# One maximum per head in the global attention branch, copies and sums moved between engines, and an output product that begins with the first tokens

## The chip, the cores and the metric

The kernel runs on one core of a Trainium2 chip. The metric is the device time of one execution in microseconds. The kernel before took 1566.17 us (median of three runs, 1564.94 to 1567.08). The engines are named as the profile names them: PE (TensorE), PEld (its weight loads), DVE (VectorE), ACT (ScalarE), POOL (GpSimd) and SP (SyncE, which here only starts DMAs).

## What is computed

One layer of a diffusion transformer over 1024 latent tokens of width 1024 with 256 context tokens. Two attention branches read the same modulated input: A, windowed over 128 neighbours with a sink logit, and B, global, with a normalisation of q and k. Each has 8 query heads in two groups of four (one key/value head per group), head size 64. A SwiGLU convolution network follows. What the change touches is branch B and the merge:

```python
def _global_attention(q, k_all, v_all):          # keys: 1024 latent + 256 context
    def one_block(i):
        q_blk = lax.dynamic_slice_in_dim(q, i * BLOCK, BLOCK, axis=1)
        p = jax.nn.softmax(_gqa_scores(q_blk, k_all), axis=-1)
        return _gqa_values(p, v_all)
...
def _merge_branches(o_a, o_b, gate_logits, w_branch_a, w_branch_b, w_out):
    g_a, g_b = jnp.split(jax.nn.sigmoid(gate_logits), 2, axis=-1)
    return (g_a * (o_a @ w_branch_a) + g_b * (o_b @ w_branch_b)) @ w_out
```

## The kernel before

All is float32. Every product of a weight with an activation is made of three matmuls on rounded halves (high and low part of each operand, `mm3`, lines 92 to 95; `split`, lines 83 to 90, makes the halves: a rounding copy and a subtraction).

The kernel is a sequence of stages: the projections and gates (to about 336 us of the profile), the attention (to about 764 us), the output product of branch B and the merge (to about 812 us), the output projection with its layer norm, and the convolution network (to the end). The attention goes over 32 units. A unit is one branch, one block of 128 query tokens and one group of four heads; units 0 to 15 are branch A, units 16 to 31 branch B (in the names of tiles, `p_6_1_3` is block 6, group 1, head 3).

A unit of branch B has two parts. The score part: `context` (lines 550 to 553) makes the scores against the 256 context keys for four heads in one PSUM tile `s_x` (`cxp`, lines 501 to 514), DVE takes their maximum (L508, L509), and ACT makes the four exponentials from PSUM (L463 with tile `p_x`). Then `lat` (lines 465 to 499) makes for each head the scores against the 1024 latent keys in another PSUM tile, DVE copies them out scaled and keeps their extreme with the context maximum as the start value (L496), and ACT makes the exponential in place. So the context part has one maximum, and the latent part another that includes it. `norm` (lines 516 to 531) brings the two together: DVE takes the difference (L520), ACT its exponential `f` (L521), POOL multiplies the four context tiles by it (L524), DVE corrects and adds the sums (L525, L526) and inverts (L531). The value part of a unit, done while the next unit makes its scores, goes over ten chunks of 128 keys: PE transposes the four heads (L568) into a PSUM tile of which there are three, ACT rounds it (L577, or a copy L574 for the two chunks whose split is on POOL), DVE subtracts (L578), PE multiplies by the values (L589, L590). `rows` (lines 533 to 544) turns the inverted sums into rows by a transpose, a DMA to DRAM and one back. `out_step` (lines 592 to 607) copies the product out (ACT, L595), moves its lower half up (POOL, L597), adds the two halves (DVE, L600, two instructions), multiplies by the inverted sums (POOL, L603) and splits the result into the tiles `O` (POOL, L87 and L90).

The score PSUM tile has two buffers (`s_tile`, line 830), used in turn by `s_x` and by the four latent heads. In units 18 to 25 the program also inserts the output product of branch A (`fill`, lines 910 to 915): four loads of weights and 16 groups of 12 matmuls (`grp`, lines 869 to 880), one per 128 output channels and half of the tokens. A program list sorts the steps of the parts by a due position (lines 918 to 923); a scheduler in the compiler framework then orders the instructions of each engine by its own estimates. Each engine runs its list strictly in order.

The output product of branch B: the weights of the first 256 channels are loaded and split in unit 31 (lines 907 to 909), and their four groups are issued after the last unit (lines 933 and 934), first half of tokens before second. The others (lines 1008 to 1020) load and split their weights after that and make, for each 128 channels, both halves of the tokens in one loop. `merge` (lines 998 to 1004) adds the branches and splits the sum; nineteen SBUF slots called `H` are handed from one use to the next (`ht`, `hput`, lines 138 to 144), a load into a slot waiting until its last reader is done.

Of the kernel before, what the change touches and what calls it, by code (L numbers as in the profile page):

```python
# [23 lines left out]
GRID = 64  # L24
LN_EPS = 1e-5
# [45 lines left out]
def layer_kernel(  # L71
# [20 lines left out]
    def mm3(ps, a, b, start, stop, resumed=False):  # L92
        nc.tensor.matmul(ps, a[0], b[0], start=start, stop=False, skip_group_check=resumed)  # L93
        nc.tensor.matmul(ps, a[0], b[1], start=False, stop=False, skip_group_check=resumed)  # L94
        nc.tensor.matmul(ps, a[1], b[0], start=False, stop=stop, skip_group_check=resumed)  # L95
# [324 lines left out]
    class Unit:  # L420
# [44 lines left out]
        def lat(self, h):  # L465
# [33 lines left out]
            self.pc[h, 0] = p  # L499

        def cxp(self):
            kh = self.br * 2 + self.g
            s = s_tile(f"s{self.id}_x")
            for h in range(4):
                self.qk(s[:, h * NC:(h + 1) * NC], h, KC[0][:, kh])
            self.other = small(f"nmc_{self.id}", (P, 4))
            self.smc = small(f"smc_{self.id}", (P, 4))
            nc.vector.reduce_max(self.other, s.rearrange("p (a b) -> p a b", a=4), axis=AX.X)  # L508
            nc.vector.tensor_tensor(out=self.other, in0=self.other, in1=self.qscale(nqs), op=ALU.mult)  # L509
            p = p_tile(f"p{self.id}_x")  # L510
            for h in range(4):
                self.pc[h, 1] = p[:, h * NC:(h + 1) * NC]
                self.soft(s[:, h * NC:(h + 1) * NC], self.pc[h, 1], h, self.other, self.smc,
                          self.qscale(pqs)[:, h:h + 1])

        def norm(self):
            hc = slice(self.g * 4, self.g * 4 + 4)
            f = small(f"f_{self.id}", (P, 4))
            if self.br:
                nc.vector.tensor_tensor(out=f, in0=self.nm, in1=self.other, op=ALU.subtract)  # L520
                nc.scalar.activation(f, f, AF.Exp)  # L521
                for h in range(4):
                    p = self.pc[h, 1]
                    nc.gpsimd.tensor_scalar(out=p, in0=p, scalar1=f[:, h:h + 1], scalar2=0.0, op0=ALU.mult, op1=ALU.add)  # L524
                nc.vector.tensor_tensor(out=self.smc, in0=self.smc, in1=f, op=ALU.mult)  # L525
                nc.vector.tensor_tensor(out=self.sm, in0=self.sm, in1=self.smc, op=ALU.add)  # L526
            else:
                nc.vector.tensor_tensor(out=f, in0=self.nm, in1=sinkb[:, hc], op=ALU.add)
                nc.scalar.activation(f, f, AF.Exp)
                nc.vector.tensor_tensor(out=self.sm, in0=self.sm, in1=f, op=ALU.add)  # L530
            nc.vector.reciprocal(self.sm, self.sm)  # L531
# [28 lines left out]
        def value_steps(self):  # L560
# [31 lines left out]
            def out_step():  # L592
# [5 lines left out]
                ot = att.tile([P, 2, P], F32, tag="ot", name=f"ot{nm}", bufs=1)  # L598
                for h in range(2):
                    nc.vector.tensor_tensor(out=ot[h * HD:(h + 1) * HD],  # L600
                                            in0=avs[0:HD].rearrange("p (a b q) -> p a b q", b=2, q=P)[:, :, h],
                                            in1=up.rearrange("p (a b q) -> p a b q", b=2, q=P)[:, :, h], op=ALU.add)
# [17 lines left out]
            steps.insert(2 - self.br, self.rows)  # L620
# [236 lines left out]
    def branch_steps(br, wsrc, halves, wpool, engs, f2s=range(4)):  # L857
# [3 lines left out]
        def ld(f2, key):  # L861
            r = wpool.tile([P, 8, P], F32, tag="wraw", name=f"rwb{br}_{key}", bufs=1)
            nc.sync.dma_start(r, wsrc[f2])
            h = wpool.tile([P, 8, P], R32, tag="whl", name=f"hwb{br}_{key}", bufs=2)
            l = wpool.tile([P, 8, P], R32, tag="whl", name=f"lwb{br}_{key}", bufs=2)
            split(r, h, l, *engs)
            w[f2] = h, l
# [14 lines left out]
        for f2 in f2s:  # L882
            steps.append(lambda f2=f2: ld(f2, f"{f2}_{halves[0]}"))
            for f in (2 * f2, 2 * f2 + 1):
                for hf in halves:
                    steps.append(lambda f=f, hf=hf: grp(f, hf, pt_tile))
# [8 lines left out]
    fill = []  # L895
    nu = len(units)
    vq = []
    for u in range(nu + 1):
# [16 lines left out]
        fs = [fill.pop(0) for _ in range(nf)]  # L915
        if u < nu:
# [15 lines left out]
    hput("KC", *[f"VT{t}" for t in range(5)])  # L932
    for st_ in first[1:]:
        st_()
# [70 lines left out]

    for f in (0, 1):
        merge(f)
    wb = {f2: weight(w_b[f2], f"wb{f2}", 8, he=nc.scalar, le=nc.vector, rtag=None) for f2 in (1, 2)}
    for f in range(2, KT):
        bT[1, f] = ht(f"bT1_{f}")  # L1010
        nc.sync.dma_start(bT[1, f], sgd[KT + f])
        w = wb[f // 2]
        ps = big(f"b1_{f}")
        for j in range(4):
            k = (f % 2) * 4 + j
            for hf in (0, 1):
                a = O[1, hf, 0, j // 2][:, j % 2], O[1, hf, 1, j // 2][:, j % 2]
                mm3(ps[:, hsl(hf)], (w[0][:, k], w[1][:, k]), a, j == 0, j == 3)
# [797 lines left out]
```

## Time and profile before

| | us |
|---|---|
| median of three runs | 1566.17 |
| the profiled execution, its own time | 1568.22 |
| its span from first to last instruction | 1566.4 |
| PE busy | 1532.0 |
| DVE busy | 1195.9 |
| ACT busy | 809.0 |
| POOL busy | 754.8 |

The profile is of one execution. Its views: busy time of each engine in chosen stretches; groups of like instructions with count, busy time, mean length in ns and the idle time of the engine just before them with what ended it; who waited for whom; the chain of work that ended last, followed back step by step; and the instructions in order of time. A matmul's row is longer than the distance to the next matmul, because matmuls overlap in the engine; so PE counts as busy in part of a short wait.

### The profile page before, as it was taken

To read this page: it belongs to the slowest core of one execution; us is meant where nothing else is said; L and a number is where in the kernel's file an instruction comes from. 1 tells how busy PE (TensorE), PEld (TensorE's weight loads), DVE (VectorE), ACT (ScalarE), POOL (GpSimd) and SP (SyncE) were. 2 spreads that over 40 slices of the span, in tenths; PEclk is the share of its full clock that TensorE was granted. 3 is DMA by queue.
4 is the path that set the end of the run, shared out by engine and by line. 5 is a ranking of instruction groups with operands and counts; after the bars stand their busy time and mean duration, and the time that the engine had idled before them with its cause. 6 is when DMAs were issued, how large, how long until landed. Compare 5 with 4: busy or idle time off the path is not lost.

```text
span 1566.4 us, 21965 instructions
## 1 busy us (share of the span) xinstructions
PE 1532.0 (98%) x7652; PEld 1269.8 (81%) x7652; DVE 1195.9 (76%) x1751; ACT 809.0 (52%) x1436; POOL 754.8 (48%) x729
## 2 busy tenths in 40 slices
PE   9999999999999999999999999999999999999997
PEld 7888888878877887777688898888888888888886
DVE  7588847548888777888674779888888888657797
ACT  5422223448888667688522565454444444435533
POOL 0374303426666556665423545666666675021063
PEclk9999999999999999999999999999999999999999
DMA  9667663322237555531452132333334446996723
GB/s 378 237 214 266 235 218 99 99 87 67 61 113 163 127 145 128 125 71 35 143 165 78 54 108 81 121 108 108 108 108 108 108 110 179 352 284 217 261 89 108
DMA packets 111874, 229.73 MB, mean 147 GB/s; under 512 B 13490, under 2 KB 27314, under 8 KB 111667
## 3 DMA queue, kind: packets, MB, share of 16 engines
q1 hardware_dynamic: 96464, 199.20, 37.9%
q0 software_dynamic: 10400, 20.19, 8.3%
q10 hardware_dynamic: 4898, 8.94, 1.5%
q8 instruction: 60, 0.98, 0.2%
q14 instruction: 52, 0.42, 0.1%
HBM read 177.09 MB, written 65.87 MB: 155 GB/s over the span
## 4 chain that ended last, share of the span: by engine, by line
PE 86%; DVE 8%; ACT 3%; issue 2%; POOL 1%; DMA 0%; DVEq 0%; ACTq 0%; POOLq 0%
PE ptr L568 5%; PE g L95 4%; PE g L94 4%; PE g L93 4%; PE p L95 4%; PE p L93 4%; PE p L94 4%; PE b L95 3%; PE b L94 3%; PE b L93 3%; PE s L450 2%; PE av L589 2%; PE c L93 2%; PE d L93 2%; PE a L93 2%; PE a L95 2%
## 5 line engine op out<-in xcount | busy, mean ns | idle before, releaser
L578 DVE TENSOR_TENSOR ptl<-ptr,pth 128x512 fp32r<-128x512 f32 x188 | 124.6, 685 | 27.9 <-ACT pth L577 25.8
L568 PE MATMUL ptr<-ident,p 128*128 128x128 f32 x816 | 127.0, 278 | 12.1 <-DVE ptl L578 9.2
L577 ACT CAST pth<-ptr 128x512 fp32r<-128x512 f32 x188 | 106.4, 588 | 57.0 <-PE ptr L568 31.1
L90 DVE TENSOR_TENSOR ld<-rd,hd 128x1024 fp32r<-128x1024 f32 x77 | 97.8, 1285 | 48.1 <-ACT hd L85 44.5
L463 ACT ACTIVATE p<-p,nm 128x1024 f32<-128x1024 f32 (+2 forms) x128 | 125.3, 981 | 9.5 <-DVE p L496 8.8
L568 PEld LDWEIGHTS ptr<-ident,p 128*128 128x128 f32 x816 | 93.7, 140 | 42.4 <-DVE ptl L578 15.8
L85 ACT CAST hd<-rd 128x1024 fp32r<-128x1024 f32 x77 | 79.6, 1051 | 85.0 <-PE p L95 62.4
L589 PE MATMUL av<-pth,VT 128*128 128x512 f32 x236 | 104.8, 444 | 1.1 <-ACT avs L595 0.5
L93 PE MATMUL p<-hd 128*128 128x512 f32 x264 | 103.2, 391 | 0.0
L95 PE MATMUL p<-hd,ld 128*128 128x512 f32 x264 | 102.7, 389 | 0.0
L94 PE MATMUL p<-ld,hd 128*128 128x512 f32 x264 | 102.7, 389 | 0.0
L95 PE MATMUL g<-hh,wlg 128*128 128x512 f32 x256 | 99.7, 390 | 0.4 <-POOL wlg L90 0.4
L93 PE MATMUL g<-hh,whg 128*128 128x512 f32 x256 | 99.9, 390 | 0.0
L94 PE MATMUL g<-hl,whg 128*128 128x512 f32 x256 | 99.6, 389 | 0.0
L590 PE MATMUL av<-ptl,VT 128*128 128x512 f32 x236 | 97.6, 413 | 2.0 <-POOL ptl L90 1.9
L496 DVE TENSOR_SCALAR_CACHE_REDUCE p<-s,cvt,nmc 128x1024 f32<-128x1024 f32 x64 | 84.5, 1340 | 12.4 <-PE s L451 12.0
L90 POOL TENSOR_TENSOR wlg<-wg,whg 128x512 fp32r<-128x512 f32 x32 | 45.3, 1421 | 99.3 <-ACT whg L85 86.4
L450 PE MATMUL s<-KL,q 128*128 128x512 f32 (+2 forms) x192 | 76.1, 396 | 2.7 <-ACT p_x L463 2.0
L87 POOL TENSOR_SCALAR pth<-prw 128x512 fp32r<-128x512 f32 x48 | 31.0, 646 | 90.9 <-ACT prw L574 64.3
L451 PE MATMUL s<-KL,q 128*128 128x512 f32 (+2 forms) x192 | 71.5, 372 | 0.0
L85 ACT CAST wS<-s 128x512 fp32r<-128x512 f32 x76 | 45.3, 620 | 49.5 <-POOL s L1149 48.7
L85 ACT CAST wA<-ru 128x512 fp32r<-128x512 f32 x57 | 35.5, 623 | 60.7 <-PE d L95 32.8
(406 smaller groups left out, 4956.2 us busy)
## 6 DMA issues: line engine op xcount, KB each, us to landing
wml<-in_wmodT_dram SPq DMA_DIRECT2D x48, 512.0 KB
ru<-in_w_up_dram SPq DMA_DIRECT2D x38, 512.0 KB
rd<-td SPq DMA_DIRECT2D x55, 256.0 KB
rd<-sd SPq DMA_DIRECT2D x44, 256.0 KB
rd<-in_w_dn_dram SPq DMA_DIRECT2D x33, 256.0 KB
wm<-in_wmodT_dram SPq DMA_DIRECT2D x16, 512.0 KB
wg<-in_w_g_dram SPq DMA_DIRECT2D x32, 256.0 KB
sgd<-sg ACTq DMA_DIRECT2D x32, 256.0 KB
```

The lines of the kernel that those rows point to most:

```text
L85: cast[:] = [nc.scalar.copy(hi, src).ins]
L90: low[:] = [lo_eng.tensor_tensor(out=lo, in0=src, in1=hi.bitcast(F32), op=ALU.subtract).ins]
L93: nc.tensor.matmul(ps, a[0], b[0], start=start, stop=False, skip_group_check=resumed)
L94: nc.tensor.matmul(ps, a[0], b[1], start=False, stop=False, skip_group_check=resumed)
L95: nc.tensor.matmul(ps, a[1], b[0], start=False, stop=stop, skip_group_check=resumed)
L450: nc.tensor.matmul(o, self.q[0][:, hs], ks, start=True, stop=False)
L463: nc.scalar.activation(p, s, AF.Exp, bias=nm[:, h:h + 1], scale=scale, accum_out=sm[:, h:h + 1])
L568: nc.tensor.transpose(tr[:, h * P:(h + 1) * P], self.pslice(h, n), ident)
L577: nc.scalar.copy(hi, tr)
L578: nc.vector.tensor_tensor(out=lo, in0=tr, in1=hi.bitcast(F32), op=ALU.subtract)
L589: nc.tensor.matmul(self.av, v, hi, start=first, stop=False)
L590: nc.tensor.matmul(self.av, v, lo, start=False, stop=self.left == 0)
```

## The change

In `cxp` the context scores are no longer reduced and exponentiated at once: four DVE instructions, one per head, copy them out of PSUM, scaled, into `p_x`, and keep each head's extreme as the start value for the latent scan. In `lat` the exponential of a head's latent scores is followed by that of its context scores, both with the head's one maximum. The correction in `norm` goes: no `f`, no multiplication on POOL. The two additions of `out_step` are on POOL in branch B. `rows` stands one step later. The weights of the first 256 channels of `w_b` are loaded two units earlier and kept in H slots, those of the next 512 are loaded during the last value part; the first group of the output product (first 512 tokens, `first[0]`) is issued within the last value part, then the second group of the first tokens, then the first-token halves of channels 256 to 511, and only then the second tokens. `mm3` returns its last instruction, so that the groups of the second tokens can be held behind it. To make slots free, the context keys `KC` are given back after the last scores.

```diff
         def lat(self, h):
...
             self.soft(p, p, h, self.nm, self.sm, -1.0)
             self.pc[h, 0] = p
+            if self.br:
+                self.soft(self.pc[h, 1], self.pc[h, 1], h, self.nm, self.smc, -1.0)
 
         def cxp(self):
...
-            nc.vector.reduce_max(self.other, s.rearrange("p (a b) -> p a b", a=4), axis=AX.X)
-            nc.vector.tensor_tensor(out=self.other, in0=self.other, in1=self.qscale(nqs), op=ALU.mult)
             p = p_tile(f"p{self.id}_x")
             for h in range(4):
-                self.pc[h, 1] = p[:, h * NC:(h + 1) * NC]
-                self.soft(s[:, h * NC:(h + 1) * NC], self.pc[h, 1], h, self.other, self.smc,
-                          self.qscale(pqs)[:, h:h + 1])
+                c = slice(h * NC, (h + 1) * NC)
+                self.pc[h, 1] = p[:, c]
+                nc.vector.tensor_scalar(out=p[:, c], in0=s[:, c], scalar1=self.qscale(nqs)[:, h:h + 1], scalar2=TOP,
+                                        op0=ALU.mult, op1=ALU.min, accum_out=self.other[:, h:h + 1])
 
         def norm(self):
             hc = slice(self.g * 4, self.g * 4 + 4)
-            f = small(f"f_{self.id}", (P, 4))
-            if self.br:
-                nc.vector.tensor_tensor(out=f, in0=self.nm, in1=self.other, op=ALU.subtract)
-                nc.scalar.activation(f, f, AF.Exp)
-                for h in range(4):
-                    p = self.pc[h, 1]
-                    nc.gpsimd.tensor_scalar(out=p, in0=p, scalar1=f[:, h:h + 1], scalar2=0.0, op0=ALU.mult, op1=ALU.add)
-                nc.vector.tensor_tensor(out=self.smc, in0=self.smc, in1=f, op=ALU.mult)
-                nc.vector.tensor_tensor(out=self.sm, in0=self.sm, in1=self.smc, op=ALU.add)
...
+            more = self.smc if self.br else small(f"f_{self.id}", (P, 4))
+            if not self.br:
+                nc.vector.tensor_tensor(out=more, in0=self.nm, in1=sinkb[:, hc], op=ALU.add)
+                nc.scalar.activation(more, more, AF.Exp)
+            nc.vector.tensor_tensor(out=self.sm, in0=self.sm, in1=more, op=ALU.add)
             nc.vector.reciprocal(self.sm, self.sm)
...
+                e = nc.gpsimd if self.br else nc.vector
                 for h in range(2):
-                    nc.vector.tensor_tensor(out=ot[h * HD:(h + 1) * HD],
+                    e.tensor_tensor(out=ot[h * HD:(h + 1) * HD],
...
-            steps.insert(2 - self.br, self.rows)
+            steps.insert(2, self.rows)
...
-            hput(f"KL{br * 2}", f"KL{br * 2 + 1}")
+            hput(f"KL{br * 2}", f"KL{br * 2 + 1}", *["KC"] * br)
...
-        if u == 31:
-            first = branch_steps(1, w_b, (0, 1), att, (nc.gpsimd, nc.gpsimd), (0,))
-            first[0]()
+        if u == 29:
+            first = branch_steps(1, w_b, (0, 1), att, (nc.gpsimd, nc.gpsimd), (0,),
+                                 lambda: [ht(f"{a}wb1_0", (P, 8, P), R32) for a in "hl"])
+            first.pop(0)()
...
+        if u == nu:
+            fs.append(first[0])
+            for f2 in (1, 2):
+                rwb[f2] = ht(f"rwb{f2}", (P, 8, P))
+                nc.sync.dma_start(rwb[f2], w_b[f2])
...
-    hput("KC", *[f"VT{t}" for t in range(5)])
-    for st_ in first[1:]:
-        st_()
+    hput(*[f"VT{t}" for t in range(5)])
+    first[2]()
...
+    wb = {}
+    for f2 in (1, 2):
+        wb[f2] = [wq.tile([P, 8, P], R32, tag="w", name=f"{a}wb{f2}", bufs=4) for a in "hl"]
+        split(rwb[f2], *wb[f2], nc.scalar, nc.vector)
+        hput(f"rwb{f2}")
+    pb = {}
+
+    def half(f, hf):
+        if f not in pb:
+            bT[1, f] = ht(f"bT1_{f}")
+            nc.sync.dma_start(bT[1, f], sgd[KT + f])
+            pb[f] = big(f"b1_{f}")
+        w = wb[f // 2]
+        for j in range(4):
+            k = (f % 2) * 4 + j
+            a = O[1, hf, 0, j // 2][:, j % 2], O[1, hf, 1, j // 2][:, j % 2]
+            i = mm3(pb[f][:, hsl(hf)], (w[0][:, k], w[1][:, k]), a, j == 0, j == 3)
+        return i
+
+    half(2, 0)
+    with tc.issue_after(half(3, 0)):
+        for n in (1, 3):
+            first[n](sml)
+    hput("hwb1_0", "lwb1_0")
     for f in (0, 1):
         merge(f)
-    wb = {f2: weight(w_b[f2], f"wb{f2}", 8, he=nc.scalar, le=nc.vector, rtag=None) for f2 in (1, 2)}
     for f in range(2, KT):
-        bT[1, f] = ht(f"bT1_{f}")
-        nc.sync.dma_start(bT[1, f], sgd[KT + f])
-        w = wb[f // 2]
-        ps = big(f"b1_{f}")
-        for j in range(4):
-            k = (f % 2) * 4 + j
-            for hf in (0, 1):
-                a = O[1, hf, 0, j // 2][:, j % 2], O[1, hf, 1, j // 2][:, j % 2]
-                mm3(ps[:, hsl(hf)], (w[0][:, k], w[1][:, k]), a, j == 0, j == 3)
+        for hf in (0, 1):
+            if f > 3 or hf:
+                half(f, hf)
+        ps = pb[f]
```

More of the change, by code (lines that the diff above doesn't have):

```diff
@@ L24 @@
 GRID = 64
+TOP = 3.0e38
 LN_EPS = 1e-5
@@ L94, in mm3 @@
         nc.tensor.matmul(ps, a[0], b[1], start=False, stop=False, skip_group_check=resumed)
-        nc.tensor.matmul(ps, a[1], b[0], start=False, stop=stop, skip_group_check=resumed)
+        return nc.tensor.matmul(ps, a[1], b[0], start=False, stop=stop, skip_group_check=resumed).ins
     const = ctx.enter_context(tc.tile_pool(name="const", bufs=1, side="left"))
@@ L855, in layer_kernel, with branch_steps @@
     bT = {}
-    def branch_steps(br, wsrc, halves, wpool, engs, f2s=range(4)):
+    def branch_steps(br, wsrc, halves, wpool, engs, f2s=range(4), hl=None):
         steps = []
@@ L863, in ld @@
             nc.sync.dma_start(r, wsrc[f2])
-            h = wpool.tile([P, 8, P], R32, tag="whl", name=f"hwb{br}_{key}", bufs=2)
-            l = wpool.tile([P, 8, P], R32, tag="whl", name=f"lwb{br}_{key}", bufs=2)
+            h, l = hl() if hl else [wpool.tile([P, 8, P], R32, tag="whl", name=f"{a}wb{br}_{key}", bufs=2) for a in "hl"]
             split(r, h, l, *engs)
@@ L885, in branch_steps @@
                 for hf in halves:
-                    steps.append(lambda f=f, hf=hf: grp(f, hf, pt_tile))
+                    steps.append(lambda mk=pt_tile, f=f, hf=hf: grp(f, hf, mk))
         return steps
@@ L892, in done @@
         if g and i == NT - 1:
-            hput(f"KL{br * 2}", f"KL{br * 2 + 1}")
-    fill = []
+            hput(f"KL{br * 2}", f"KL{br * 2 + 1}", *["KC"] * br)
+    fill, rwb = [], {}
     nu = len(units)
```

8 lines of the change are left out of this document (2 added, 6 removed).

## The prediction

> **What bounds the kernel now.** I read the page first, for the engine and the chain, then the attention of branch B in stages.
>
> ```profile
> span 1566.4 us, 21965 instructions
> PE 1532.0 (98%) x7652; PEld 1269.8 (81%) x7652; DVE 1195.9 (76%) x1751; ACT 809.0 (52%) x1436; POOL 754.8 (48%) x729
> ...
> PE 86%; DVE 8%; ACT 3%; issue 2%; POOL 1%; DMA 0%; DVEq 0%; ACTq 0%; POOLq 0%
> ```
>
> PE is busy for 98% of the span and is 86% of the chain that ended last. The change takes no matmul away, so it can only remove PE's waits, and only where it acts. The starts of the context scores mark the units; here are units 18, 26 and 31 (first start of `s_x` in each row).
>
> ```profile
> L450 PE MATMUL s_x<-KC,q x4: 278/280/282, 489.7 to 490.4; 128*128 128x256 f32 x4
> ...
> L450 PE MATMUL s_x<-KC,q x4: 281/283/283, 654.7 to 655.4; 128*128 128x256 f32 x4
> ...
> L450 PE MATMUL s_x<-KC,q x4: 278/280/282, 736.6 to 737.3; 128*128 128x256 f32 x4
> ```
>
> The table by stage, cut at these starts (units 16 and 17; 18 to 25, which carry the output product of branch A; 26 to 30; unit 31 and the tail):
>
> ```profile
> 461.10:489.70 28.60, 25.49 (x147) 19.65 (x148) 24.06 (x43) 24.49 (x59) 20.71 (x30) 1.00 0.82 198
> 489.70:654.70 165.00, 161.91 (x905) 132.37 (x904) 122.38 (x214) 112.53 (x245) 96.10 (x130) 1.00 0.56 131
> 654.70:736.60 81.90, 75.14 (x442) 59.65 (x441) 72.04 (x117) 64.84 (x146) 48.81 (x70) 1.00 0.27 64
> 736.60:785.00 48.40, 44.84 (x233) 35.07 (x232) 33.78 (x56) 26.86 (x53) 21.48 (x31) 1.00 0.37 126
> ```
>
> The columns are length, then busy time of PE, PEld, DVE, ACT, POOL. PE is idle for 3.1, 3.1, 6.8 and 3.6 us, 16.5 in all: that is most of what can be won. A matmul row hides a little more:
>
> ```profile
> 770.13 0.40 PE L94 MATMUL b<-O,hwb 128*128 128x512 f32 x1
> ...
> 770.36 0.39 PE L95 MATMUL b<-O,lwb 128*128 128x512 f32 x1
> ```
>
> Rows are 0.39 us long and 0.23 apart, so each wait is up to 0.16 us longer than the idle time shown.
>
> Units 26 to 30 take 81.9 / 5 = 16.4 us each. In units 18 to 25 the fill adds 16 groups of 12 matmuls, 192 x 0.2275 = 43.7 us, so a unit without it costs (165.0 - 43.7) / 8 = 15.2 us. The same work is 1.2 us dearer where no fill matmuls stand in the gaps; DVE is busy there for 72.0 of 81.9 us (88%). What PE waits for, and what DVE spends, in units 26 to 30 (groups):
>
> ```profile
> L496 DVE TENSOR_SCALAR_CACHE_REDUCE p<-s,cvt,nmc 128x1024 f32<-128x1024 f32 x20 | 26.4, 1339 | 5.5 <-PE s L451 5.5
> L568 PE MATMUL ptr<-ident,p 128*128 128x128 f32 x160 | 24.2, 277 | 5.1 <-DVE ptl L578 4.7 <-ACT q L443 0.4
> L463 ACT ACTIVATE p<-p,nm 128x1024 f32<-128x1024 f32 x19 | 21.9, 1154 | 3.0 <-DVE p L496 2.7
> L450 PE MATMUL s<-KL,q 128*128 128x512 f32 x40 | 16.4, 409 | 1.6 <-ACT p_x L463 1.6
> L463 ACT ACTIVATE p_x<-s_x,nmc,cvt 128x256 f32<-128x256 f32 x20 | 11.1, 569 | 2.7 <-DVE nmc L509 2.7
> L524 POOL TENSOR_SCALAR p_x<-p_x,f 128x256 f32<-128x256 f32 x20 | 9.4, 524 | 2.3 <-ACT f L521 2.3
> L600 DVE TENSOR_TENSOR ot<-avs,up 64x256 f32<-64x256 f32 x10 | 8.3, 832 | 0.3 <-POOL up L597 0.3
> L508 DVE TENSOR_REDUCE nmc<-s_x 128x4 f32<-128x1024 f32 x5 | 6.1, 1218 | 1.6 <-PE s_x L451 1.6
> L525 DVE TENSOR_TENSOR smc<-smc,f 128x4 f32<-128x4 f32 x4 | 2.5, 617 | 0.0
> L520 DVE TENSOR_TENSOR f<-nm,nmc 128x4 f32<-128x4 f32 x4 | 1.8, 456 | 0.0
> ```
>
> PE's 6.8 us are 4.7 for DVE's subtraction (which frees the transposes' PSUM tile), 1.6 for the context exponentials (which hold the score PSUM tile) and 0.4 for a cast. The chain in these units passes through work that the change removes:
>
> ```profile
> 692.02 2.31 ACT p_x L463 x8
> ...
> 705.72 1.85 DVE smc L525
> ...
> 725.31 2.15 ACT p_x L463 x7
> ```
>
> So ACT's block of four context exponentials, and a 128x4 DVE instruction that took 1.85 us, stood on the path.
>
> **The change, part by part.** *DVE per unit of B.* Removed: 8.3 + 6.1 + 2.5 + 1.8 = 18.7 us in five units, 3.7 each. Added: four 128x256 scans from PSUM. No such row exists; the nearest are the 1024 scan above (1339 ns) and the 640 scan:
>
> ```profile
> L496 DVE TENSOR_SCALAR_CACHE_REDUCE p<-s,negsink 128x640 f32<-128x640 f32 x48 | 41.1, 874 | 1.3 <-PE s L451 0.9 <-PE ptr L568 0.4
> ```
>
> The slope is (1339 - 874) / 384 = 1.21 ns per element, which gives 408 ns for 256: four are 1.6 us. Bounds are 4 x 1339 / 4 = 1.3 us (no fixed cost) and 4 x 874 = 3.5 us. I take 1.6, as the two rows lie on a line through almost zero. DVE then does 72.0 / 5 - 3.7 + 1.6 = 12.3 us per unit, 81% of a 15.2 us unit instead of 88% of 16.4. What is queued behind the four scans on DVE is the previous unit's subtractions (chunks 8 and 9) and this unit's first latent scan; they stand behind L508 and L509 today, so the extra hold is 1.6 - 1.2 = 0.4 us, covered while PE still has matmuls of chunks 5 to 9 in its list.
>
> *The two additions on POOL.* The subtraction of two 128x512 inputs and the product of two 128x256 inputs bound a 64x256 addition:
>
> ```profile
> L90 POOL TENSOR_TENSOR ptl<-prw,pth 128x512 fp32r<-128x512 f32 x48 | 63.1, 1315 | 2.6
> ...
> L603 POOL TENSOR_TENSOR ot<-ot,rb 128x256 f32<-128x256 f32 x32 | 24.0, 749 | 11.0 <-DVE ot L600 10.7
> ```
>
> I take 0.75 us each, 1.5 per unit (ends 0.75, if 64 partitions cost half, and 2.6). The four context products go (9.4 / 5 = 1.9 us), so POOL does 0.4 us less; POOL also no longer waits for DVE in the middle (10.7 us over the kernel). On DVE these additions depend on what POOL does beside them:
>
> ```profile
> 681.31 1.28 POOL L90 TENSOR_TENSOR ptl<-prw,pth 128x512 fp32r<-128x512 f32 x1
> 681.43 1.87 DVE L600 TENSOR_TENSOR ot<-avs,up 64x256 f32<-64x256 f32 x2
> ...
> 745.86 0.85 DVE L600 TENSOR_TENSOR ot<-avs,up 64x256 f32<-64x256 f32 x2 [0.26 <-POOL up L597]
> ```
>
> The pair took 1.87 us beside a POOL subtraction and 0.85 us without one. That is the size of the stall that leaves DVE. The Trainium skill ("SBUF — State Buffer", Who interferes with whom) says that a DVE instruction with two SBUF inputs contends with a GpSimd one that reads SBUF, and one with a PSUM input does not; these rows agree. Against the change, the Trainium skill ("Perfetto Trace Analysis", Optimizing Scalar/DVE Operations) says that moving work between these two engines might not help, since they share a read port. By that rule the 8.3 us of L600 would come back as longer DVE instructions, DVE would save 0.4 us per unit instead of 2.1, so of PE's 4.7 us for DVE 0.9 would go beside the 1.6 for ACT: 2.5 of 6.3, and my sum would shrink to -8.5 x 0.4 - 2.5 = -5.9. I weigh it low: after the change the B part of DVE's list has only the 128x4 sum (L526) with both inputs in SBUF.
>
> *ACT.* Four 256-wide exponentials from SBUF replace four from PSUM (569 ns). The 640 wide row gives the slope:
>
> ```profile
> L463 ACT ACTIVATE p<-p,nm 128x640 f32<-128x640 f32 x48 | 40.0, 838 | 0.3 <-DVE p L496 0.3
> ```
>
> (1154 - 838) / 384 = 0.82 ns, so 522 ns; ends 289 (1154 / 4) and 838. ACT's sum hardly changes (-0.2 us per unit), its place does: no block of 2.3 us at the unit's start, and the score PSUM tile is free after DVE's 1.6 us instead of after DVE's 1.2 and ACT's 2.3, 1.9 us earlier.
>
> *What this is worth.* Units 26 to 30: I take them to the 15.2 us that units 18 to 25 reach, 5 x 1.2 = -6.0 us (ends 0 and -6.8 with the hidden share on top). Units 16 and 17 have the same work and 3.1 us of idle PE: half, -1.5 (0 to -3.1). Units 18 to 25: a third of 3.1 idle, -1.0 (0 to -3.1). ACT is the next late engine: 64.8 / 5 = 13.0 us in a 15.2 us unit, 85%.
>
> *Tail.* PE's waits from unit 31 on:
>
> ```profile
> PE ptr L568 <- DVE ptl L578: 1.0, 2, 0.7
> PE b L95 <- DVE lwb L90: 0.9, 1, 0.9
> PE b L93 <- DVE bT L880: 0.9, 1, 0.9
> PE av L590 <- POOL ptl L90: 0.4, 1, 0.4
> PE b L94 <- POOL O L90: 0.2, 1, 0.2
> ```
>
> The early group (12 matmuls, 2.7 us) stands among the last unit's transposes and covers the 1.0 and 0.4. Three groups of the first tokens (8.2 us) now lie between the last value matmul and the first that reads the last `O`; that path is a copy, four POOL steps and about 4 us, so the 0.2 goes, and so does the 0.9 for the PSUM tile of `bT`. The 0.9 for `lwb` stays: in the built order DVE still multiplies the second group's result before it subtracts the weights, and only five matmuls bridge it. Sum -2.5 (ends +1.5, if the bridge is short by the 1.28 us of one subtraction more, and -3.6).
>
> *Queues and loads.* In the built order two 512 KB weight loads move ahead on SP, one before the denominator rows of the last four units, one before those of the last two. A load into a slot waits for its readers and holds those rows up; today's largest such wait in the tail is
>
> ```profile
> SPq L961 <- POOL O L90: 2.2, 1, 2.2
> ```
>
> The rows have most of a unit to spare, so I cost this at nothing; without that cover it is 2.2 us. `rows` one step later and the slots of `KC` cost nothing for the same reason. From 785 us on the work is the same.
>
> Sum: -6.0 - 1.5 - 1.0 - 2.5 = -11.0 us. The profiled execution took 1568.2 us (span 1566.4 and 1.8 around it), which gives 1557.2; the median of the runs, 1566.2, lies 2.0 below it, which gives **1555**.
>
> **Rivals.** *All of PE's idle time goes:* -16.5 and some 20 waits of 0.16 hidden, -3: 1546.7. For it: nearly every listed wait is for something that is shortened. Against: units 18 to 25 still show 3.1 us.
>
> *The wait only moves:* transposes wait for the subtraction, that for ACT's cast, that for PE; with three PSUM tiles the loop may be as slow with a lighter DVE. Only the tail is left, -2.5: 1563.7. Against: DVE's 88%.
>
> *Slower: ACT falls behind at the unit's end.* Per head ACT must now do 1154 + 522 = 1.68 us against a DVE scan of 1.34, so after two scans back to back it is 0.34 late, and the last context exponential (0.52 and its read-out of 0.21) stands before the next unit's first cast: 1.07 us per unit.
>
> ```profile
> L463 ACT ACTIVATION_READ_ACCUMULATOR p_x<-s_x,nmc,cvt 128x1 f32 x20 | 4.2, 208 | 0.0
> ```
>
> It decides from the point where PE has under about 1 us of other work between the last head's exponential and the next unit's first transposes. Against: the eight context matmuls and the last chunks stand there. If it holds in all 16 units, +17.1 and none of the -8.5 in the units but the tail's -2.5: 1580.8.
>
> **How the numbers follow.** Forecast 0.60 (1549 to 1562), all idle gone 0.14, wait moves 0.13, slower 0.13. A measurement tells 0.2%, 3.1 us, from no change, so 1563.7 counts as the same. Faster 0.74, same 0.13, slower 0.13. The range 1546 to 1566 takes in the first three and leaves out the slower one and the edges.
>
> **What would show it.** Right: units 26 to 30 near 76 us together, PE's wait for `ptl` under 2 us there and none for `p_x`; scans of about 0.41 us; POOL additions of 0.75; DVE busy near 12.3 us per unit; ptl waits gone in the tail and about 1 us for `lwb` left. Wrong: first transposes of a unit waiting for ACT, SP holding the denominator rows, or 256-wide scans near 0.8 us.

## The result, and the profile after

The changed kernel takes **1552.46 us** (median of four runs, 1551.07 to 1555.59), the kernel before, beside it, 1565.86. The ratio is 0.9917, 95% interval 0.9900 to 0.9934: 13 us faster (10 to 16). The forecast was 1555, with 1546 to 1566. The profiled execution took 1552.42 us, 1.8 more than its span; first the page, span and busy time:

```profile
span 1550.6 us, 21959 instructions
...
PE 1526.3 (98%) x7652; PEld 1269.6 (82%) x7652; DVE 1164.9 (75%) x1783; ACT 802.1 (52%) x1420; POOL 753.1 (49%) x697
```

The number of matmuls is the same. The table by stage, cut at the same places as before: length, then busy time of PE, PEld, DVE, ACT, POOL.

```profile
460.40:487.50 27.10, 25.68 (x146) 19.77 (x147) 24.78 (x55) 23.01 (x53) 20.12 (x26) 1.00 0.87 209
487.50:649.70 162.20, 160.07 (x905) 132.32 (x904) 111.02 (x227) 108.67 (x240) 95.36 (x115) 1.00 0.53 122
649.70:722.70 73.00, 72.60 (x443) 60.03 (x443) 59.89 (x128) 63.12 (x140) 44.44 (x59) 1.00 0.43 98
722.70:768.20 45.50, 43.99 (x233) 35.08 (x232) 27.43 (x49) 24.93 (x52) 23.18 (x30) 1.00 0.39 135
```

Units 16 and 17 went from 28.6 to 27.1 us, units 18 to 25 from 165.0 to 162.2, units 26 to 30 from 81.9 to 73.0. There PE is now idle for 0.4 us where it was idle for 6.8, and a unit takes 14.6 us instead of 16.4. From unit 31 to the first matmul of the output projection it is 71.5 us instead of 74.4. That is 16.1 us in the parts that the change touches. The two profiled executions differ by 15.8 us (1568.22 and 1552.42), the medians by 13.4: the profiled execution of the kernel before lies 2.4 us above the median of its runs, that of the changed kernel does not (see the last experiment below). From the first output matmul on the changed kernel takes 1.0 us more (756.4 instead of 755.4).

What PE waited for in the changed kernel, in units 18 to 25, in units 26 to 30, from unit 31 on, and around the start of the output projection (in us: total, times, longest; each kernel has line numbers of its own):

```profile
PE s L451 <- DVE p_x L515: 1.1, 1, 1.1
PE av L583 <- ACT pth L571: 0.9, 1, 0.9
...
PE ptr L562 <- ACT q L444: 0.3, 1, 0.3
...
PE b L94 <- DVE bT L874: 0.9, 1, 0.9
PE ptr L562 <- DVE ptl L572: 0.5, 1, 0.5
...
PE y L94 <- ACT mh L86: 1.1, 1, 1.1
PE y L95 <- DVE ml L91: 0.8, 1, 0.8
```

In units 26 to 30 the 4.7 us for `ptl` and the 1.6 us for `p_x` are gone. The groups there:

```profile
L497 DVE TENSOR_SCALAR_CACHE_REDUCE p<-s,cvt,nmc 128x1024 f32<-128x1024 f32 x20 | 26.5, 1338 | 3.3 <-PE ptr L562 3.3
L572 DVE TENSOR_TENSOR ptl<-ptr,pth 128x512 fp32r<-128x512 f32 x39 | 25.7, 684 | 8.5 <-ACT pth L571 8.2
...
L464 ACT ACTIVATE p_x<-p_x,nm 128x256 f32<-128x256 f32 x19 | 9.4, 497 | 0.0
L515 DVE TENSOR_SCALAR_CACHE_REDUCE p_x<-s_x,cvt 128x256 f32<-128x256 f32 x20 | 8.6, 480 | 1.3 <-PE s_x L452 1.2
...
L595 POOL TENSOR_TENSOR ot<-avs,up 64x256 f32<-64x256 f32 x10 | 7.3, 735 | 0.7
```

DVE now stands idle for 8.2 us until ACT's casts come (1.9 us in the kernel before): it follows, it does not lead.

**Where the tile was held.** The theory that the comparison suggests, and that the forecast had only in passing, is that the score PSUM tile of the context was taken too long. One unit of the kernel before, in order of time (start, length, engine, line):

```profile
688.62 1.23 DVE L508 TENSOR_REDUCE nmc<-s_x 128x4 f32<-128x1024 f32 x1 [0.80 <-PE s_x L451]
...
689.84 0.68 DVE L578 TENSOR_TENSOR ptl<-ptr,pth 128x512 fp32r<-128x512 f32 x1
...
690.75 0.68 DVE L578 TENSOR_TENSOR ptl<-ptr,pth 128x512 fp32r<-128x512 f32 x1
...
691.43 0.12 DVE L509 TENSOR_TENSOR nmc<-nmc,cvt 128x4 f32<-128x4 f32 x1
...
692.02 0.57 ACT L463 ACTIVATE p_x<-s_x,nmc,cvt 128x256 f32<-128x256 f32 x1
...
693.65 0.57 ACT L463 ACTIVATE p_x<-s_x,nmc,cvt 128x256 f32<-128x256 f32 x1
...
694.37 0.50 PE L450 MATMUL s<-KL,q 128*128 128x512 f32 x1 [0.81 <-ACT p_x L463]
```

The maximum is ready at 689.85, but the small product L509 stands on DVE behind two subtractions (and an addition and a reciprocal that are not shown) until 691.43, and only then can ACT's four exponentials run. Head 1's scores wait for the tile until 694.37. I call the time from the end of the last context matmul to the end of the last read of the tile the hold. It is 5.7 us here and 5.6 on average over units 26 to 30. The forecast counted 3.5 (1.2 + 2.3), without the queue before L509. In a unit of the changed kernel (`s_x` complete at 693.20) the first and the last copy are

```profile
693.23 0.48 DVE L515 TENSOR_SCALAR_CACHE_REDUCE p_x<-s_x,cvt 128x256 f32<-128x256 f32 x1
...
695.80 0.47 DVE L515 TENSOR_SCALAR_CACHE_REDUCE p_x<-s_x,cvt 128x256 f32<-128x256 f32 x1
```

a hold of 3.1 us; the average over units 26 to 30 is 2.3. The rival theory is the forecast's own emphasis: DVE was too busy (88%), and longer still because its additions met POOL's subtractions.

### The profile page after: what moved, and what is told of

Read it like the earlier page. It is cut to its first block, busy times and chain, and to the rows that moved or that the text cites. A ratio compares the mean times of both kernels' runs of the same rounds, so it can differ in the third digit from the quotient of the medians.

```text
span 1550.6 us, 21959 instructions
## 1 busy us (share of the span) xinstructions
PE 1526.3 (98%) x7652; PEld 1269.6 (82%) x7652; DVE 1164.9 (75%) x1783; ACT 802.1 (52%) x1420; POOL 753.1 (49%) x697
## 5 line engine op out<-in xcount | busy, mean ns | idle before, releaser
L572 DVE TENSOR_TENSOR ptl<-ptr,pth 128x512 fp32r<-128x512 f32 x188 | 123.5, 685 | 32.6 <-ACT pth L571 31.8
L497 DVE TENSOR_SCALAR_CACHE_REDUCE p<-s,cvt,nmc 128x1024 f32<-128x1024 f32 x64 | 84.6, 1339 | 7.4 <-PE ptr L562 5.5
```

Source lines behind the costliest of these rows:

```text
L497: nc.vector.tensor_scalar(out=p, in0=o, scalar1=self.qscale(nqs)[:, hs] if self.br else -1.0, scalar2=self.other[:, hs], op0=ALU.mult, op1 ...
L572: nc.vector.tensor_tensor(out=lo, in0=tr, in1=hi.bitcast(F32), op=ALU.subtract)
```

## The experiments

All twelve in one table, beside the kernel before and the changed one: ratio to the kernel before on the same chip with its interval, then the stages of the profile in us (units 16 and 17; 18 to 25; 26 to 30; unit 31 to the first output matmul) and the mean hold in units 26 to 30.

| kernel | ratio (95%) | 16-17 | 18-25 | 26-30 | 31 to output | hold |
|---|---|---|---|---|---|---|
| before | 1 | 28.6 | 165.0 | 81.9 | 74.4 | 5.6 |
| before again | one run | 28.6 | 165.0 | 82.0 | 74.4 | 5.6 |
| changed | 0.9917 (0.9900-0.9934) | 27.1 | 162.2 | 73.0 | 71.5 | 2.3 |
| context alone | 0.9969 (0.9958-0.9980) | 27.8 | 165.6 | 77.0 | 76.1 | 3.1 |
| sums alone | 0.9989 (0.9981-0.9998) | 28.6 | 162.0 | 80.2 | 77.7 | 5.6 |
| output product alone | 0.9980 (0.9972-0.9989) | 28.6 | 166.0 | 79.5 | 70.9 | 5.1 |
| rows later alone | 0.9983 (0.9974-0.9991) | 27.7 | 165.4 | 80.6 | 76.3 | 5.8 |
| copy only | 0.9958 (0.9944-0.9972) | 28.9 | 164.7 | 73.5 | 75.4 | 2.7 |
| changed, context undone | 0.9988 (0.9978-0.9997) | 27.6 | 166.2 | 79.5 | 71.3 | 5.6 |
| changed, sums on DVE | 0.9919 (0.9905-0.9933) | 27.1 | 161.3 | 76.8 | 72.5 | 2.2 |
| changed, sums of A on POOL too | 0.9977 (0.9967-0.9987) | 28.7 | 163.0 | 72.6 | 71.6 | 2.2 |
| changed, tile held | 0.9945 (0.9930-0.9960) | 25.8 | 161.8 | 76.5 | 73.2 | 8.1 |
| changed, tile not held (control) | 0.9912 (0.9899-0.9926) | 27.3 | 160.1 | 72.4 | 72.1 | 2.2 |
| changed, `lwo` late | 0.9917 (0.9904-0.9930) | 27.1 | 161.8 | 72.9 | 71.5 | 2.3 |

**Context alone**, on the kernel before: the hunks of `cxp`, `lat` and `norm`.

```diff
+            if self.br:
+                self.soft(self.pc[h, 1], self.pc[h, 1], h, self.nm, self.smc, -1.0)
...
-                self.soft(s[:, h * NC:(h + 1) * NC], self.pc[h, 1], h, self.other, self.smc,
-                          self.qscale(pqs)[:, h:h + 1])
+                nc.vector.tensor_scalar(out=p[:, c], in0=s[:, c], scalar1=self.qscale(nqs)[:, h:h + 1], scalar2=TOP,
+                                        op0=ALU.mult, op1=ALU.min, accum_out=self.other[:, h:h + 1])
```

> The kernel before with the context part alone (one maximum, four DVE copies out of PSUM, no correction). Two theories of the 13.2 us that units 16 to 31 lost. Release theory: what mattered is that the score PSUM tile of the context comes free without ACT's block of exponentials; then this edit alone brings 9 us or more (time below 1557). DVE-load theory: what mattered is DVE's work, made long by its contention with POOL; this edit leaves DVE's sum nearly as it is (10.4 us removed in five units, 4 x 480 ns x 5 = 9.6 us added), so it brings under 4 us, about what PE waited for p_x (1.6 us in units 26 to 30, some 3 in all): 1562 to 1564, and the waits for ptl stay near 4.7 us in units 26 to 30.

Measured: 1561.49 us, 4.9 us gained by the ratio: between the two theories. The units say more than the sum. Units 26 and 27 held the tile for 4.1 and 3.9 us and took 16.8 and 16.2 us; units 28 to 30 held it for 2.4 and took 14.9, 14.9 and 14.3. Where the hold is short the units are as short as in the changed kernel, and the gain in units 26 to 30 (4.9 us) is partly given back from unit 31 on (1.7).

**Sums alone**, on the kernel before.

```diff
+                e = nc.gpsimd if self.br else nc.vector
                 for h in range(2):
-                    nc.vector.tensor_tensor(out=ot[h * HD:(h + 1) * HD],
+                    e.tensor_tensor(out=ot[h * HD:(h + 1) * HD],
```

> The kernel before with the two additions of the output halves on POOL alone. DVE-load theory: DVE loses 8.3 us in units 26 to 30, the pair that stood beside POOL's subtractions, and PE's 4.7 us for ptl there go for the greater part: 8 us or more in all, below 1558. Release theory: the wait for p_x stays and the loop between subtraction, cast and PE is as slow: under 3 us, 1563 to 1566. A third way: POOL gets the additions on top of the four context products that it keeps here (48.8 + 7.4 of 81.9 us), the denominators and O come later, and nothing is won.

Measured: 1564.88 us, 1.7 us gained. The DVE-load theory fails as stated: units 26 to 30 shorten by 1.7 us with the hold as long as before, and what units 18 to 25 gain (3.0) is lost again from unit 31 on (3.3). Part of what DVE gave away also came back. These rows of its units 26 to 30 stand against 617 and 456 ns before:

```profile
L525 DVE TENSOR_TENSOR smc<-smc,f 128x4 f32<-128x4 f32 x4 | 4.9, 1224 | 0.0
L520 DVE TENSOR_TENSOR f<-nm,nmc 128x4 f32<-128x4 f32 x4 | 2.7, 681 | 0.0
```

That is 3.3 us more than the 4.3 before, against 8.3 removed. Four of these eight instructions took 1 us or more, against two of eight before, and each of the six ran beside a POOL subtraction. The rule that the forecast weighed (the Trainium skill, "Perfetto Trace Analysis", Optimizing Scalar/DVE Operations: moving work between the two might not help) thus holds for two fifths of it here, if all of the 3.3 us is put down to the move. In the changed kernel these small instructions no longer exist, and its rows L497 and L572 (1338 and 684 ns) are no longer than before.

**Output product alone**, on the kernel before: all that the change does to the order of branch B's output product and its loads.

```diff
-        if u == 31:
+        if u == 29:
...
+        if u == nu:
+            fs.append(first[0])
...
+    half(2, 0)
+    with tc.issue_after(half(3, 0)):
+        for n in (1, 3):
+            first[n](sml)
```

> The kernel before with the changed order of the output product alone (early weights, first tokens first). The forecast gave this part -2.5 us. By the trace of the changed kernel unit 31 to the first output matmul came out 2.9 us shorter and 1.0 was given back: -1.9, 1564.0. A rival: the shortening there belongs to the lighter DVE of the last unit, and this order brings nothing or costs the 1.0: 1566 to 1567.

Measured: 1563.76 us, 3.1 us gained, and 3.5 in the stage from unit 31 to the output projection. So this part stands by itself, a little above the forecast's 2.5. The rival (that a lighter DVE did it) fails. Its units 26 to 30 are also 2.4 us shorter and units 18 to 25 1.0 us longer, though the edit does no more in them than move a weight load and its split to unit 29; that is not explained here.

**Rows later alone**, on the kernel before.

```diff
-            steps.insert(2 - self.br, self.rows)
+            steps.insert(2, self.rows)
```

> The kernel before with only the transposed sums (rows) one step later in the value part of branch B. The forecast cost it at nothing: within 1 us of 1565.9. A rival: the later transpose no longer stands at the point where DVE's reciprocal ends last (PE waited 0.3 us for it in units 16 and 17), which would be worth 0.3 us in each of 16 units at most: 1561 to 1565.

Measured: 1563.93 us, 2.7 us gained by the ratio, but nothing in the profile: its four stages add up to 350.0 us, as before (349.9). In units 26 to 30 the waits changed places: 0.9 us for `ptl` where it was 4.7, but 4.1 us for `p_x` where it was 1.6. So a wait can move here, though not round the loop that the forecast's rival "the wait only moves" names. Its profiled execution is shorter in parts that the edit does not touch: 458.7 us before unit 16 and 753.2 from the first output matmul on, where the two executions of the kernel before took 459.0 and 461.1, and 755.1 and 755.4. Where the 2.7 us of the ratio come from stays open.

**Copy only**, on the kernel before: the early release without the single maximum.

```diff
-            nc.vector.reduce_max(self.other, s.rearrange("p (a b) -> p a b", a=4), axis=AX.X)
-            nc.vector.tensor_tensor(out=self.other, in0=self.other, in1=self.qscale(nqs), op=ALU.mult)
...
-                self.soft(s[:, h * NC:(h + 1) * NC], self.pc[h, 1], h, self.other, self.smc,
-                          self.qscale(pqs)[:, h:h + 1])
+                nc.vector.tensor_scalar(out=p[:, c], in0=s[:, c], scalar1=self.qscale(nqs)[:, h:h + 1], scalar2=TOP,
+                                        op0=ALU.mult, op1=ALU.min, accum_out=self.other[:, h:h + 1])
+            for h in range(4):
+                self.soft(self.pc[h, 1], self.pc[h, 1], h, self.other, self.smc, -1.0)
```

> The kernel before, but DVE copies the four context scores out of PSUM (as in the change) and ACT's four exponentials read the copy, still as one block at the start of the unit, with their own maximum and with the correction on POOL. It parts the two things that the context edit does. Release theory: what paid there (units 28 to 30 at 14.9 us with PE busy without a gap, 16.4 before) is that the score PSUM tile is free after DVE instead of after ACT; then these units stay near 15 us here and the time is near that of the context edit, 1561 to 1562.5, although DVE does 0.7 us more per unit. Block theory: what paid is that ACT's block of 2.3 us no longer stands between the first latent scans and their exponentials; then PE's wait for p_x goes here too but returns as a wait for a cast or the first latent exponential, units stay near 16 us, and the time is 1565 to 1568.

Measured: 1561.53 us, 6.6 us gained: no less than the whole context part (4.9, with intervals that overlap), so that on this base no gain shows for the single maximum itself. Its units 26 to 30, and below them those of the kernel with the sums alone:

```profile
653.70:727.10 73.40, 72.42 (x442) 59.53 (x441) 65.95 (x144) 63.22 (x144) 48.41 (x70) 1.00 0.31 72
...
649.10:729.30 80.20, 74.53 (x443) 59.48 (x442) 66.28 (x106) 65.03 (x146) 56.71 (x82) 1.00 0.30 68
```

These rows decide against the DVE-load theory. With the copy DVE is busy for 66.0 of 73.4 us, 90%, a larger share than the 88% before; ACT's block, the correction on POOL and the additions on DVE are all still there; and yet PE is idle for 1.0 us and the units take 14.7 us. DVE's busy time did fall from 72.0 us, in part since its additions ran shorter (624 ns instead of 832). But the kernel with the sums alone has as little of it (66.3 us) and needs 16.0 us a unit. So DVE's share of 88% was not the bound, and the early copy is what pays. The copy frees the tile early, and it also takes the maximum with its small product out of the way of ACT's exponentials; the pair that holds the tile, below, parts these two.

**Changed, context undone.** The first experiment's hunks, taken back from the changed kernel.

```diff
-            if self.br:
-                self.soft(self.pc[h, 1], self.pc[h, 1], h, self.nm, self.smc, -1.0)
...
+                self.soft(s[:, h * NC:(h + 1) * NC], self.pc[h, 1], h, self.other, self.smc,
+                          self.qscale(pqs)[:, h:h + 1])
```

> The changed kernel with the context part put back to that of before (maximum by DVE, exponentials from PSUM as a block, correction on POOL). The four parts tried alone brought 4.9 (context), 1.7 (sums), 3.1 (order of the output product) and 2.7 us (rows later) by their ratios, 12.4 together, where the whole brought 13. If they add: 1552.5 + 5 = 1557 to 1558.5, and units 26 to 30 near 15.9 us. If the context part is what lets the others pay (their waits end in the wait for p_x otherwise): 1560 or more, and p_x waits of 3 us or more in units 26 to 30.

Measured: 1565.13 us: only 1.9 us of the 13 are left. Its units 26 to 30 in the table by stage:

```profile
652.30:731.70 79.40, 74.62 (x442) 60.45 (x441) 60.48 (x106) 64.51 (x146) 52.94 (x78) 1.00 0.40 90
```

and what PE waited for there:

```profile
PE s L451 <- ACT p_x L464: 3.6, 4, 1.0
PE ptr L569 <- DVE sm L527: 0.7, 1, 0.7
```

The opposite of the copy: DVE is busy for 76%, 60.5 us and so nearly as little as in the changed kernel (59.9), and the units still take 15.9 us; the largest of PE's waits is the one for `p_x`. So the parts do not add. The context part is worth 4.9 us on the kernel before and 11 in the changed kernel.

**Changed, sums on DVE.**

```diff
-                e = nc.gpsimd if self.br else nc.vector
                 for h in range(2):
-                    e.tensor_tensor(out=ot[h * HD:(h + 1) * HD],
...
+                    nc.vector.tensor_tensor(out=ot[h * HD:(h + 1) * HD],
```

> The changed kernel with the two additions back on DVE. If the parts add: 1552.5 + 1.7 = 1554 to 1555, mostly lost in units 18 to 25 (3.0 us there when tried alone). DVE-load theory: with the context part in place DVE is the next late engine and the contention shows, +4 us or more: 1556.5 or more, with waits for ptl back in units 26 to 30. If ACT is the next late engine: no loss, 1552 to 1553.5.

Measured: 1554.09 us. By the times the sums are worth 0.3 us, with intervals that allow some 3 either way; by the profile units 26 to 30 lose 3.8 us (76.8 against 73.0), and units 18 to 25 gain 0.9. What they cost on DVE there:

```profile
L594 DVE TENSOR_TENSOR ot<-avs,up 64x256 f32<-64x256 f32 x10 | 4.2, 418 | 5.0 <-POOL up L591 5.0
```

The pair takes 0.84 us a unit, without the contention of before (832 ns each). But DVE stands with them at the head of its queue for 1 us a unit until POOL's copy `up` has come. A latent scan is next in the queue, and PE waits for it (2.7 us in three places):

```profile
656.54 0.85 DVE L594 TENSOR_TENSOR ot<-avs,up 64x256 f32<-64x256 f32 x2 [1.42 <-POOL up L591]
657.42 1.34 DVE L497 TENSOR_SCALAR_CACHE_REDUCE p<-s,cvt,nmc 128x1024 f32<-128x1024 f32 x1
```

PE's scores of the next head start at 658.83, as this scan ends. So what the move to POOL takes away is a wait in order more than a contention. Its worth in time is not settled.

**Changed, tile held, and its control.** One small ACT instruction more per unit; its result is not used. In the first it reads the context scores in PSUM, in the control the copied ones.

```diff
                 self.soft(self.pc[h, 1], self.pc[h, 1], h, self.nm, self.smc, -1.0)
+                if h == 0:
+                    nc.scalar.activation(small(f"jk_{self.id}", (P, 4)), self.sx[:, 0:4], AF.Exp, bias=self.nm[:, 0:1],
+                                         scale=0.0)
```

> The changed kernel with one small ACT instruction more per unit of branch B (128x4): it reads four columns of the context scores in PSUM, with the maximum of head 0 as its bias, so that the score tile stays taken until after head 0's scan. Its result is not used. Release theory: the hold after the last context matmul goes from 2.3 us back to 5 or more, units 26 to 30 go from 14.6 towards 16 us each, and the loss in all is 5 us or more: 1557.5 to 1565. DVE-load theory: DVE is as light as in the changed kernel, so nothing is lost but the small instruction, 0.2 us on ACT: 1552 to 1554.

> The control: the same small ACT instruction reads four columns of the copied scores in SBUF, so the tile is not held. Both theories: within 2 us of the changed kernel (1552.5), hold 2.3 us, units 26 to 30 near 14.6 us. If it loses as much as the kernel that holds the tile, then what costs is the additional instruction in ACT's list and the release theory has no support from that run.

Measured: 1556.32 and 1551.20 us. The instruction itself costs nothing that shows; that it holds the tile costs 5.1 us between the medians. In the kernel that holds the tile, the instruction, and two of PE's waits in units 26 to 30:

```profile
L504 ACT ACTIVATE jk<-s_x,nm 128x4 f32<-128x4 f32 x5 | 1.2, 243 | 0.0
...
PE av L586 <- ACT pth L574: 1.1, 2, 0.6
...
PE s L451 <- ACT jk L504: 0.2, 1, 0.2
```

1.2 us of ACT in five units, and units 26 to 30 are 4.1 us longer than the control's. So the early release is shown to be worth that much. Yet the hold is 8.1 us, longer than before, a unit takes 15.3, not 16.4, and the time stays short of the 1557.5 or more that the release theory expected: the hold alone gives back about half. PE waits for the tile itself for only 0.2 us; the rest of its idle time there (2.6 us in all, 0.3 in the control) stands at other waits. The other half belongs to what else the old context part has in the lists (the queue before L509, ACT's block) or to the order that the scheduler builds around a longer hold; these runs do not part that further.

**Changed, sums of branch A on POOL too.**

```diff
-                e = nc.gpsimd if self.br else nc.vector
+                e = nc.gpsimd
```

> The changed kernel with the additions on POOL in branch A too (units 0 to 15; one line). DVE is busy for 108.5 of 124.4 us there and PE idle for 5.1; the 26 additions cost DVE 14.0 us, POOL has 46 us free. If DVE's load binds there: 2 us or more won, 1548 to 1551. If the reciprocal that waits for ACT's f (11.2 us of DVE's idle time) or the loop of subtraction and cast binds: within 1 us of 1552.5.

Measured: 1562.69 us: nine us lost by the ratio, which neither theory had. The part before unit 16 took 470.1 us instead of 460.4; PE's longest wait from 336 us to there is

```profile
PE av L584 <- POOL ptl L91: 7.7, 9, 0.9
```

and the additions are, in the groups of that stretch,

```profile
L595 POOL TENSOR_TENSOR ot<-avs,up 64x256 f32<-64x256 f32 x26 | 18.9, 729 | 1.0
```

From 336 us to unit 16 the changed kernel shows no wait of PE for POOL. POOL was free for 46 us of the 124 from 336 us to unit 16 in the changed kernel, but a chunk's split on POOL now stands behind 1.5 us of additions, and PE needs that chunk.

**Changed, `lwo` late.** In the changed kernel DVE stood for 6.46 us with the subtraction `lwo` at the head of its queue, until its data had come, and I put the new waits at the output projection down to that.

```diff
     for f in (0, 1):
         merge(f)
+    late = low[0]
...
+            with tc.issue_after(late):
+                wout_start(f // 2 - 2, None)
```

> The changed kernel with the subtraction of the first output weights (lwo) queued on DVE behind the first two merges. In the changed kernel it stood at the head of DVE's queue for 6.5 us until its weights had come, the products of the second tokens and the merges behind it came late, and PE waited 1.9 us for mh and ml at the output product. If that queue is the cause: these waits go, 1.0 us from the last value matmul to the first output matmul and after it: 1551 to 1552. If the merges are late for another reason (PE's groups of the second tokens come last), nothing changes: 1552.5.

Measured: 1551.39 us, ratio as that of the changed kernel. The products behind it now start at 763.99 instead of 765.97, but the waits are still there:

```profile
PE y L94 <- ACT mh L86: 1.2, 1, 1.2
...
PE y L95 <- DVE ml L91: 0.8, 1, 0.8
```

My explanation fails. A better one is in the table by stage of the changed kernel:

```profile
764.80:789.20 24.40, 24.40 (x109) 20.21 (x108) 24.21 (x20) 7.38 (x7) 8.82 (x10) 1.00 0.46 155
```

DVE works for 24.2 of 24.4 us: with PE's groups of the second tokens in a row, all merges fall into one stretch, and DVE's list reaches the last one late. That was argued from the trace, not tried.

**Before again**, the kernel unchanged.

> The kernel before once more, for a second profile: how far the stages differ from one execution to the next. The parts before unit 16 and behind the first output matmul, which no edit touches, differed by up to 2.8 us between profiles; I expect as much here, and less than 1 us in units 26 to 30 (81.9 in the first).

Its profiled execution took 1565.84 us, 2.4 less than the first. The four stages agree within 0.1 us; the part before unit 16 took 459.0 instead of 461.1, and the changed kernel's 460.4 lies between them. So in these two executions the stages tell a us where times do not, and 2.4 of the 15.8 us between the first two profiled executions are what the first had above a usual one, most of it in a part that no edit touches.

## Why the prediction came out as it did

The direction, the range and the main place were right; the forecast was 2.5 us too high, and its account of the cause was half wrong. That the time came so near is in part luck: the stages gained 16.1 us where the sum had 11.0. Against that, 1.0 us was given back at the output projection, and the 2.0 us that the forecast took off for the median did not come (profiled 1552.42, median 1552.46).

- *Units 26 to 30, -6.0:* -8.9. The step "I take them to the 15.2 us that units 18 to 25 reach" was mis-sized: with no gap left PE needs 14.5 us a unit (72.6 / 5). The 0.2275 us a matmul behind the 15.2 stands in no row; the 0.23 of the rows shown would give 15.1.
- *DVE as the bound:* wrong as the cause. "DVE is busy there for 72.0 of 81.9 us (88%)" carried the argument; the copy alone ran at 90% without the waits, and the changed kernel without its context part at 76% with a wait for `p_x`. The 4.7 us that the list of waits puts down to DVE's subtraction went when the tile was released.
- *"The score PSUM tile is free ... 1.9 us earlier":* the right mechanism, 3.4 us by the trace (5.64 to 2.27), and not priced as a term of its own. The forecast had the subtractions "behind L508 and L509"; in the unit shown two of them stand ahead of L509. By the pair that holds the tile it is worth about half of what units 26 to 30 gained; what the other half is stays open.
- *Sizes:* 128x256 scans 480 ns (forecast 408, bounds 335 to 874); POOL's additions 735 (750); ACT's exponentials from SBUF 497 (522); DVE 12.0 us a unit (12.3). All near.
- *Units 16 and 17, -1.5:* -1.5. *Units 18 to 25, -1.0:* -2.8, mis-sized.
- *Tail, -2.5:* -2.9, but the two terms changed places. The wait for `lwb` that was to stay is gone, the `ptl` wait that was to go still shows 0.5, and the 0.9 for `bT` that was to go is still there: the group of channels 256 to 383 waits for its PSUM bank until DVE has multiplied the group before it.

```profile
755.68 0.47 PE L94 MATMUL b<-O,hwb 128*128 128x512 f32 x1 [0.88 <-DVE bT L874]
```

- *"From 785 us on the work is the same":* the work is, the waits are not: 1.9 us at the output projection where the kernel before showed 0.6 for `ml`.
- *`rows` and the loads cost nothing:* in the changed kernel no stage is longer than before, and PE waited for no denominator row. Alone, `rows` moved time between stages (1.3 us less in units 26 to 30, 1.9 more from unit 31 on) and left their sum as it was.
- *Rivals:* "All of PE's idle time goes" came true in units 26 to 30 alone. "The wait only moves" comes near in time without the context part (1565.13), but by a wait for `p_x`, not for a cast. ACT did not fall behind: 0.3 us of PE's waiting there ends with it.

## What to carry to other kernels

Before an engine's busy share is taken for the bound, look at how long each PSUM tile is held, and at what its last reader waits for in its own queue: here a cheap 128x4 instruction, queued between two readers, had a large part in stretching a hold from 3.5 to 5.6 us. A copy that lets a scarce tile go pays even when the engine that copies is the busiest one after PE (90% here). Parts of a change need not add: try each alone and each taken out, since here the same part was worth 5 us on one base and 11 on the other.

## What was not expected of the hardware

DVE's 128x4 additions and products can take over ten times their usual length beside a POOL subtraction. Two such instructions in the kernel before, each in two units, and the POOL subtraction beside the first:

```profile
657.17 2.40 POOL L90 TENSOR_TENSOR lwb<-rwb,hwb 128x1024 fp32r<-128x1024 f32 x1
657.38 2.21 DVE L509 TENSOR_TENSOR nmc<-nmc,cvt 128x4 f32<-128x4 f32 x1
...
673.78 0.15 DVE L509 TENSOR_TENSOR nmc<-nmc,cvt 128x4 f32<-128x4 f32 x1
...
689.76 0.15 DVE L525 TENSOR_TENSOR smc<-smc,f 128x4 f32<-128x4 f32 x1
...
705.64 1.93 DVE L525 TENSOR_TENSOR smc<-smc,f 128x4 f32<-128x4 f32 x1
```

L509 at 657.38 ends within 0.02 us of POOL's subtraction; at 673.78 POOL is at its products L524, and the same instruction takes 0.15 us. L525 takes 0.15 us beside L524 at 689.76, and 1.93 at 705.64, where POOL ends a subtraction and then makes four L524 of 0.7 us each (0.48 in most units); where POOL had the additions as well L525 averaged 1224 ns over four instructions. The Trainium skill ("SBUF — State Buffer", Who interferes with whom) says that a DVE instruction with two SBUF inputs contends with a GpSimd one that reads SBUF. These have two, and beside POOL's subtractions the trace agrees; beside L524 alone, which reads SBUF as well, L525 took no more than 0.15 to 0.29 us.

A scan of 128x256 out of PSUM with its running extreme took 480 ns, 0.36 of the 1338 ns of the scan four times as wide, so that a fixed cost of some 190 ns (an estimate: 480 - 858 / 3, from these two rows) shows, which the 640 and 1024 wide rows did not give away.
